# A hybrid retention and S5 step on one core: half of the input tiles transposed by DMA, and five smaller moves in the order of work

## The chip, the core and the metric

One core of one Trainium2 chip runs the whole kernel in one launch. The metric is the device time of one execution in microseconds (us), given as the median of several executions. The core has five engines, each with its own in-order queue: TensorE (PE; its weight loads are shown apart as PEld), VectorE (DVE), ScalarE (ACT), GpSimd (POOL) and SyncE (SP), which issues nearly all DMAs here. The 16 DMA engines are shared by all DMAs.

## The reference, cut to what matters

One layer of a streaming encoder. A prompt of 2048 rows and 8 x 16 sample rows, 1024 wide, give 17 tiles of 128 rows (tile 16 holds the samples).

```python
hn = rmsnorm(x, norm_g)
q, k, v, g_ret, u, g_ssm = split(hn @ w_in)            # 1024 x 3072
q, k = rotary(q), rotary(k) * 128 ** -0.5
o, ret_state = retention(q, k, v, ret_s0)              # 4 heads of 128, per-head decay
o = rmsnorm(o, ret_norm_g) * silu(g_ret)
y, ssm_state = s5(u, h0, ...)                          # 512 channels, complex diagonal state, scan
z = gelu(y)
z = z * sigmoid(z @ w_glu + b_glu)
z = z * silu(g_ssm)
out = rmsnorm(x + concat([o, z]) @ w_out, final_norm_g)
```

## The kernel before

Matrix products are made in fp16 with both operands split in a high and a low part: three matmuls (high x high, high x low, low x high) stand for one fp32 product. So each operand is first scaled, rounded to fp16 (the high part) and subtracted from its fp32 value (the low part).

**The order of the work** is written out by hand. A list `stream` holds *slots*, small packets of matmuls for TensorE, and `hook(i, f)` hangs any other work behind slot i. The loop at the end of the kernel runs through the slots, issues each and then its hooks, so a hook's number decides where its instructions stand in every engine's in-order queue. Waits between engines are put in by the framework; moving a hook changes only the order.

**The stages**, in slots:

1. Start (lines 319 to 633): loads, squares and scales of the first weights (`gu`), tiles 0 and 1 of x.
2. *u* (slots 0 to 167): `add_ug(False, gu)` computes the S5 input u, transposed, for six chunks of tiles: (0, 1), (2, 3), (4, 5), (6, 7, 8), (9 to 12), (13 to 16). Each chunk has four column blocks `cb`, each of eight slots of three matmuls over all rows of the chunk (256, 256, 256, 384, 512, 512 columns). `evac` scales a block out of PSUM into a buffer of `ubuf` (VectorE for even `cb`, ScalarE for odd) and leaves a DMA to DRAM (`ud`) that is issued some slots later; its pieces are the 4-byte columns of the chunk, 33 x 4 = 132 bytes for chunk 0, 128 for chunks 1 and 2, 192, 256 and 288 for the others.
3. Head 0 (slots 168 to 303), then the gate columns `gd` (to 495, as in stage 2, through SiLU), then heads 1 to 3 (136 slots each, to `G0` = 904). A head runs over tiles 0 to 8, 16, 9 to 15; `Step` projects a tile (eight slots of three matmuls), rotates q and k, multiplies scores with the mask into `sm` (`r2`, slot n + 17), and takes `sm` up again in `r3` (or, for the sample tile, `r3s` at n + 19 and four `state` calls from n + 20).
4. The S5 scan of 16 pairs of groups is hung between the slots from 286 on (`C1` = 304, one pair per 34 slots). It reads `ud`, keeps its tiles in the pool `s5` ("E5", "gw", "Vs", "dh" and others) and writes y to `yd`.
5. GLU (64 slots from `G0`): eight `Glu` objects, each 280 columns for all four blocks: `split` z, matmuls, `tanh` on ScalarE, `gate`.
6. Output (`Out`, lines 1423 to 1440): 17 tiles of two halves of 24 matmuls.

**The x tiles.** `Hn` loads a tile into its place in `R1a` (tiles 0 to 8) or `R1b` (9 to 16). `stat` squares it on ScalarE and takes the rsqrt on POOL; `norm` scales it in place on VectorE; each `half` transposes four 128 x 128 blocks on TensorE (L157) into PSUM, copies the high part out on ScalarE (L161) and the low part on VectorE (L162). `prep(t, i, lat)` hangs stat at slot i, norm at i + 4, the halves at i + lat and two later. Tiles 9 to 12 have their halves at slots 68 to 94, tiles 13 to 16 at 106 to 130; chunk 4 begins at slot 104, chunk 5 at 136.

**Weights.** A `Group` squares its weights (L194, L196), and `pre` (L215, VectorE), `mat` (L219, TensorE) and `fin` (VectorE) make scales of the norms; `Ws.split` makes the fp16 parts (L188, L189).

**The S5 set-up** (`s5_setup`, a generator) makes the tables of the scan: first some 200 small VectorE operations, then eight batches `b4` with matmuls into "kps" (L569) and transposes into "wps" (L584). `pump(setup)` runs one step of it; 180 calls are spread evenly over slots 20 to 290 (`SP0`), and by slot 290 it has to be done.

**Buffers.** `xp` has two tiles "x" of 128 x 1024 fp32, `ubp` four tiles "ub". In the u stage even chunks put two blocks into one "x" tile, odd chunks one block into one "ub". The gate columns and the S5 output use "ub" alone. A tile that is taken again waits for the DMA that last read it.

Of the kernel before, what the change touches and what calls it, by code (L numbers as in the profile page):

```python
# [10 lines left out]
F32 = mybir.dt.float32  # L11
# [9 lines left out]
D = 1024  # L21
NK = 8
# [40 lines left out]
def kernel(ctx: ExitStack, tc: tile.TileContext, eye, cst, rot, x_prompt, x_sample, state_ret,  # L63
# [71 lines left out]
    class Hn:  # L135
# [14 lines left out]
        def norm(self):  # L150
            V.tensor_scalar(self.x, self.x, self.s[:, 2:3], None, OP.mult)

        def half(self, q, bank="aux"):
# [473 lines left out]
    gu.square(6)  # L627
    gu.square(7, True)
    hns[1].half(0, "aux")
    gu.scale()  # L630
    hns[1].half(1, "tr")
    wu[0].split()
    wu[1].split()
# [16 lines left out]

    xh = [None]

    def ubuf(ci, cb, gate):
        if gate or ci % 2:
            return ubp.tile([128, 576], F32, tag="ub", name="ub", bufs=4)
        if cb % 2 == 0:
            xh[0] = xp.tile([128, D], F32, tag="x", name="xu", bufs=2)
        return xh[0][:, 512 * (cb % 2):512 * (cb % 2) + 512]

# [161 lines left out]
    def hook(i, f):  # L821
        hooks.setdefault(max(int(i), 0), []).append(f)
# [64 lines left out]
    for s in seq:  # L887
        n = s.at
        hook(n + 7, s.r0)
        hook(n + 15, s.r1)  # L890
        hook(n + 17, s.r2)
        if s.t < 16:
            hook(n + 23, s.r3)
            hook(n + 28, s.r4)
            hook(n + 32, s.st)
        else:
            hook(n, s.r3s_load)
            hook(n + 19, s.r3s)
            hook(n + 25, s.r3s2)
            for q in range(4):  # L900
                hook(n + 20 + 2 * q, lambda s=s, q=q: s.state(q))
            hook(n + 30, s.r4)
            hook(n + 33, s.st)
# [16 lines left out]
    hook(9, rest_smalls)  # L920
    for t, i, lat in ((4, 7, 10), (5, 12, 14), (6, 24, 22), (7, 32, 20), (8, 40, 20),
                      (9, 50, 18), (10, 58, 18), (11, 66, 18), (12, 76, 16), (13, 86, 20), (14, 96, 18), (15, 104, 18), (16, 112, 16)):
        prep(t, i, lat)
    for i in range(5):
        t, n = 4 * i, 1 if i == 4 else 4
        hook(64 + 14 * i, lambda t=t, n=n: dma(rots[:, t:t + n, :], dap(rot, t * 16384, [[128, 128], [16384, n], [1, 128]])))
# [286 lines left out]
    for i in range(1, len(groups)):  # L1213
        grp = groups[i][0]
        _, f0, l0 = groups[i - 1]
        if i == 1:
            ld, sq, sc, sp_ = 9, 46, 88, [98 + 8 * k for k in range(8)]
        else:
            ld, sq, sc, sp_ = f0 + 8, f0 + 20, f0 + 64, [f0 + 78 + 7 * k for k in range(8)]
        for k in range(8):  # L1220
            hook(ld + (4 if i == 1 else 5) * k, grp.ws[k].load)
            hook(sq + 5 * k, lambda grp=grp, k=k: grp.square(k))
            hook(sp_[k], grp.ws[k].split)
        hook(sc, grp.pre)
        hook(sc + 4, grp.mat)
        hook(sc + 6, grp.fin)
    H3 = groups[-1][1]
    pieces = [(hf, k) for k in range(NK) for hf in range(2)]
    for j, (hf, k) in enumerate(pieces):
        hook(H3 + 4 + 3 * j, wog.sq[hf][k].load)  # L1230
        hook(H3 + 14 + 3 * j, lambda hf=hf, k=k: wog.square(hf, k))
    hook(H3 + 64, wog.pre)
    hook(H3 + 68, wog.mat)
    hook(H3 + 70, wog.norms)
    for k in range(4):
        hook(H3 + 64 + 3 * k, wgl[k].load)
        hook(H3 + 76 + 3 * k, lambda k=k: gg_.square(k, k % 2))
    hook(H3 + 88, gg_.pre)
    hook(H3 + 92, gg_.mat)
# [13 lines left out]
    class Glu:  # L1253
# [3 lines left out]
        def loadg(self):  # L1257
            t = self.t
            self.g = zp.tile([128, 1120], F32, tag="i1", name="gt", bufs=3).rearrange("p (c n) -> p c n", c=4)
            dma(self.g, dap(gd, t * NCOL + 1, [[8 * NCOL, 128], [128 * 8 * NCOL, 4], [1, 280]]))  # L1260

# [23 lines left out]
        def gate(self, cb):  # L1285
            th = self.th[cb]
            z = zb[:, cb, self.t, :]
            V.scalar_tensor_tensor(th, th, 1.0, z, op0=OP.add, op1=OP.mult)  # L1288
            G.tensor_tensor(z, th, self.g[:, cb, :], OP.mult)

# [9 lines left out]
    for t in range(8):  # L1300
        if t < 6:
            hook(G0 + 8 * t + 7, glus[t + 2].split)
        hook(G0 + (1, 1, 2, 18, 25, 31, 37, 44)[t], glus[t].loadg)
    for t in range(8):
        for cb in range(4):
            n = G0 + 8 * t + 2 * cb + 1
            hook(n, lambda t=t, cb=cb: glus[t].tanh(cb))
            hook(n + (10, 9, 7, 5, 4, 3, 1, 0)[t], lambda t=t, cb=cb: glus[t].gate(cb))

    class Out:  # L1310
# [17 lines left out]
        def split(self):  # L1328
            t = self.t
            if t > 0:  # L1330
                self.split_o()
# [68 lines left out]
    for t in range(8):  # L1400
        for k in range(NK):
            def slot(t=t, k=k):
                glus[t].mmul(k)
            stream.append(slot)
    zp = None
    for i, slot in enumerate(stream):
        if i == G0:
# [3 lines left out]
        for f in hooks.pop(i, ()):  # L1411
            f()
        if 20 <= i < SP0 and (i - 20) * 180 // (SP0 - 20) != (i - 19) * 180 // (SP0 - 20):
            pump(setup)
# [6 lines left out]
    dma(fg, dap(final_g, 0, [[0, 128], [1, D]]))  # L1421

    outs[0].split()
    for t in range(17):
# [6 lines left out]
        if t == 0:  # L1431
            outs[0].part(0, 0, 512, range(4))
            outs[0].part(1, 512, 1024, range(4))
        outs[t].mmul(0, 0, 512, 0 if t else 4)
        outs[t].mmul(1, 512, 1024, 0 if t else 4)
        if t > 0:
# [34 lines left out]
```

## Time and profile before

| | |
|---|---|
| median of 3 runs | 987.54 us (986.79 to 992.88) |
| the profiled execution | 983.05 us, span of its instructions 981.3 us |
| mean granted TensorE clock | 0.982 |
| TensorE busy | 941.1 us, 96% |
| VectorE, ScalarE, GpSimd busy | 637.4, 452.2, 341.6 us |
| DMA moved | 106.17 MB |
| u stage on TensorE (first L694 to first L708) | 19.44 to 140.19 us |
| GLU on TensorE (first L1276 to first L1356) | 745.64 to 796.75 us |

Times in views are us from the start of the span. A line of the timeline reads: start, duration, engine, source line, operation, out<-in by the program's names, shape, count; in square brackets the idle time of the engine before it and who ended it. A line of groups gives busy us and mean ns after the bar, then idle time before them. A line of waits gives the sum in us, how often, and the longest. A line of stretches gives for each engine the busy us and instructions, then the granted clock (1.00 is full speed), the DMA engines' busy share (above 1 where packets queue up) and GB/s. The chain of waits is followed back from the last instruction to whatever released each one. Matmul durations are modelled and overlap; the distance of two starts is their pace.

### The profile page before, as it was taken

How to read it: one execution, taken by the hardware profiler on the slowest of the kernel's cores; microseconds unless marked ns; L12 is line 12 of the kernel's file. 1: busy time of each engine (PE TensorE's matmuls, PEld its weight loads, DVE VectorE, ACT ScalarE, POOL GpSimd, SP SyncE). 2: the span in 40 equal slices, each digit the busy share in tenths (PEclk: the TensorE clock that was granted, in tenths of full speed). 3: DMA queues.
4: the chain of work that ended last, by engine and by line, in shares of the span. 5: the costliest groups of instructions: out<-in, count | busy, mean ns of one | idle time of the engine just before them, and what ended most of it. 6: DMA issues, size and time to landing. Idle time of an engine off the chain costs nothing.

```text
span 981.3 us, 16034 instructions
## 1 busy us (share of the span) xinstructions
PE 941.1 (96%) x5414; PEld 566.8 (58%) x5414; DVE 637.4 (65%) x1544; ACT 452.2 (46%) x1150; POOL 341.6 (35%) x636
## 2 busy tenths in 40 slices
PE   5989999999989999999999999999999999999997
PEld 4865545555677555655665556565657754444444
DVE  5598654555599746775677647777465995545544
ACT  5556324333477444543545444454445754334332
POOL 1114324421354424543555434555222760000000
PEclk7989999999999999999999989999999999999999
DMA  9995354211285334211132201273264333443432
GB/s 293 231 130 93 94 117 118 76 52 50 53 161 98 98 86 112 77 56 56 37 98 73 70 26 56 86 251 123 58 192 132 103 132 108 139 130 110 153 114 86
DMA packets 145650, 106.17 MB, mean 108 GB/s; under 512 B 62192, under 2 KB 129312, under 8 KB 145056
## 3 DMA queue, kind: packets, MB, share of 16 engines
q1 hardware_dynamic: 145424, 104.88, 40.3%
q8 instruction: 43, 0.70, 0.3%
q14 instruction: 39, 0.32, 0.1%
q10 hardware_dynamic: 144, 0.26, 0.1%
HBM read 69.15 MB, written 35.96 MB: 107 GB/s over the span
## 4 chain that ended last, share of the span: by engine, by line
PE 77%; DVE 12%; ACT 3%; issue 3%; POOL 2%; DMA 2%; SPq 1%; POOLq 0%; ACTq 0%; DVEq 0%
PE pj L708 10%; PE pj L709 10%; PE pj L710 10%; PE outps L1358 6%; PE outps L1357 6%; PE outps L1356 6%; PE ups L694 5%; PE ups L696 5%; PE ups L695 5%; DVE th L1288 2%; PE yps L1068 1%; PE scps L745 1%; PE ops L769 1%; PE yps L1070 1%; PE stps L768 1%
## 5 line engine op out<-in xcount | busy, mean ns | idle before, releaser
L725 POOL TENSOR_TENSOR rot<-A,Pm 128x128 f32<-128x128 f32 x136 | 75.4, 573 | 139.7 <-DVE A L721 110.7
L708 PE MATMUL pj<-w,R1a 128*128 128x512 f16 x288 | 109.3, 380 | 0.0
L710 PE MATMUL pj<-w,R1a 128*128 128x512 f16 x288 | 109.1, 379 | 0.0
L709 PE MATMUL pj<-w,R1a 128*128 128x512 f16 x288 | 109.1, 379 | 0.0
L1358 PE MATMUL outps<-w,mh 128*128 128x512 f16 (+1 forms) x280 | 104.4, 373 | 1.6 <-DVE mh L1326 1.6
L1356 PE MATMUL outps<-w,mh 128*128 128x512 f16 (+1 forms) x280 | 104.4, 373 | 0.0
L1357 PE MATMUL outps<-w,mh 128*128 128x512 f16 (+1 forms) x280 | 104.4, 373 | 0.0
L708 PE MATMUL pj<-w,R1b 128*128 128x512 f16 x256 | 97.7, 382 | 0.0
L709 PE MATMUL pj<-w,R1b 128*128 128x512 f16 x256 | 97.3, 380 | 0.0
L710 PE MATMUL pj<-w,R1b 128*128 128x512 f16 x256 | 97.3, 380 | 0.0
L728 ACT ACTIVATE vt<-pj,hv 128x128 f32<-128x128 f32 x68 | 25.1, 370 | 133.9 <-DVE A L721 133.9
L694 PE MATMUL ups<-R1a,w 128*128 128x256 f16 (+1 forms) x256 | 75.4, 294 | 1.5 <-ACT w L188 1.3
L696 PE MATMUL ups<-R1a,w 128*128 128x256 f16 (+1 forms) x256 | 75.2, 294 | 0.2 <-DVE w L189 0.2
L695 PE MATMUL ups<-R1a,w 128*128 128x256 f16 (+1 forms) x256 | 75.3, 294 | 0.0
L1367 ACT ACTIVATE res<-xo 128x512 f32<-128x512 f32 (+1 forms) x35 | 21.7, 619 | 107.0 <-DVE xo L1366 58.2
L132 POOL TENSOR_TENSOR ss<-ss,C 128x1 f32<-128x1 f32 x68 | 15.4, 226 | 141.8 <-ACT sj L755 141.8
L758 DVE SCALAR_TENSOR_TENSOR on<-ops,ss,gg 128x128 f32<-128x128 f32 x64 | 22.4, 350 | 62.1 <-POOL ss L133 62.1
L1366 DVE SCALAR_TENSOR_TENSOR xo<-outps,ex,xo 128x512 f32<-128x512 f32 (+1 forms) x35 | 25.6, 731 | 53.6 <-PE outps L1358 53.6
L755 ACT ACTIVATE sj<-ops 128x128 bf16<-128x128 f32 x64 | 17.7, 277 | 83.8 <-PE ops L769 81.4
L132 POOL TENSOR_TENSOR fs<-fs,half__73 128x1 f32<-128x1 f32 x16 | 3.0, 189 | 151.5 <-DVE fs L1371 151.5
L189 DVE SCALAR_TENSOR_TENSOR w<-raw,gc,w 128x512 f16<-128x512 f32 x48 | 41.1, 860 | 21.7 <-ACT w L188 21.6
L696 PEld LDWEIGHTS <-w 128*128 128x128 f16 x384 | 38.2, 99 | 22.9 <-issue 0.7
(347 smaller groups left out, 2418.1 us busy)
## 6 DMA issues: line engine op xcount, KB each, us to landing
raw<-in_w_in_dram SPq DMA_DIRECT2D x48, 256.0 KB
raw<-in_w_out_dram SPq DMA_DIRECT2D x32, 256.0 KB
xo<-in_x_prompt_dram SPq DMA_DIRECT2D x16, 512.0 KB
out_dram<-res SPq DMA_DIRECT2D x16, 512.0 KB
R1a<-in_x_prompt_dram SPq DMA_DIRECT2D x9, 512.0 KB
uraw<-ud SPq DMA_DIRECT2D x32, 140.5 KB
yd<-ysb SPq DMA_DIRECT2D x32, 140.0 KB
R1a<-yd SPq DMA_DIRECT2D x4, 1120.0 KB
```

Source lines behind the costliest of these rows:

```text
L189: V.scalar_tensor_tensor(d[:, 1, :], self.raw, sc, d[:, 0, :], op0=OP.mult, op1=OP.subtract)
L694: mm(ov, w[:, 0, c], hh, start=k == 0, stop=False)
L695: mm(ov, w[:, 0, c], hl, start=False, stop=False)
L696: mm(ov, w[:, 1, c], hh, start=False, stop=k == NK - 1)
L708: mm(self.pj, hh, w[:, 0, :], start=k == 0, stop=False)
L709: mm(self.pj, hh, w[:, 1, :], start=False, stop=False)
L710: mm(self.pj, hl, w[:, 0, :], start=False, stop=k == NK - 1)
L725: G.tensor_tensor(self.rot[:, :, a, :], A[:, :, a, :], Pm[:, :, 1 - a, :], OP.add if a else OP.subtract)
L1356: mm(p, m[:, k, 0, :], w[:, 0, cw], start=k == 0, stop=False)
L1357: mm(p, m[:, k, 0, :], w[:, 1, cw], start=False, stop=False)
L1358: mm(p, m[:, k, 1, :], w[:, 0, cw], start=False, stop=k == NK - 1)
L1366: V.scalar_tensor_tensor(self.x[:, c], p, icc, self.x[:, c], op0=OP.mult, op1=OP.add)
```

## The change

1. **Tiles 9 to 16.** No norm in place and no transposes on TensorE. `halves` scales and splits the tile by rows into a tile `b` of the "x" tag (high part on ScalarE, low part on VectorE, the scale of the norm applied in both); `turn` issues one DMA on SP that transposes `b` (128 x 2048 fp16, sixteen 128 x 128 blocks) into the tile's place in `R1a` or `R1b`. Hung at stat + 4 and stat + 8; the stats are up to eight slots earlier than before.
2. **Buffers of u.** `b` takes the "x" tiles, so all u blocks go through the four "ub" tiles.
3. **Start.** `gu.scale()` stands ahead of the first transposes of tile 1, `wu[0].split()` ahead of the second ones.
4. **Set-up later.** 30 of the 180 calls between slots 20 and 104, 150 between 104 and 290.
5. **Sample step and norms.** `r3s` and the `state` calls one slot later; `pre` of the groups two to six slots earlier, apart from `mat` and `fin`.
6. **GLU and output.** The loaded gate g is multiplied by z on POOL ahead of the tanh (`zg`, two operations of 560 columns for each t), so that the gate after the tanh is one VectorE operation that writes z. g is loaded by two DMAs, for t = 0 and 1 up to 15 slots earlier into tiles of the pool `s5`. The gates are hung closer behind their tanh. Output tile 1 has its o part split and multiplied ahead, together with tile 0's, before the z parts.

```diff
+        def halves(self):
+            b = self.b = xp.tile([128, NK, 2, 128], F16, tag="x", name="xb", bufs=2)
+            xv = self.x.rearrange("p (k n) -> p k n", k=NK)
+            rs = self.s[:, 2:3]
+            act(b[:, :, 0, :], xv, AF.Copy, scale=rs)
+            V.scalar_tensor_tensor(b[:, :, 1, :], xv, rs, b[:, :, 0, :], op0=OP.mult, op1=OP.subtract)
+
+        def turn(self):
+            nc.sync.dma_start_transpose(R(self.t).rearrange("p k l n -> p (k l) n"), self.b.rearrange("p k l n -> p (k l n)"))
...
+    gu.scale()
     hns[1].half(0, "aux")
-    gu.scale()
+    wu[0].split()
     hns[1].half(1, "tr")
-    wu[0].split()
     wu[1].split()
...
     def ubuf(ci, cb, gate):
-        if gate or ci % 2:
-            return ubp.tile([128, 576], F32, tag="ub", name="ub", bufs=4)
-        if cb % 2 == 0:
-            xh[0] = xp.tile([128, D], F32, tag="x", name="xu", bufs=2)
-        return xh[0][:, 512 * (cb % 2):512 * (cb % 2) + 512]
+        return ubp.tile([128, 576], F32, tag="ub", name="ub", bufs=4)
...
-            hook(n + 19, s.r3s)
+            hook(n + 20, s.r3s)
             hook(n + 25, s.r3s2)
             for q in range(4):
-                hook(n + 20 + 2 * q, lambda s=s, q=q: s.state(q))
+                hook(n + 21 + 2 * q, lambda s=s, q=q: s.state(q))
...
-    for t, i, lat in ((4, 7, 10), (5, 12, 14), (6, 24, 22), (7, 32, 20), (8, 40, 20),
-                      (9, 50, 18), (10, 58, 18), (11, 66, 18), (12, 76, 16), (13, 86, 20), (14, 96, 18), (15, 104, 18), (16, 112, 16)):
+    for t, i, lat in ((4, 7, 10), (5, 12, 14), (6, 24, 22), (7, 32, 20), (8, 40, 20)):
         prep(t, i, lat)
+    for t, i in ((9, 50), (10, 56), (11, 62), (12, 68), (13, 80), (14, 88), (15, 96), (16, 104)):
+        hook(i, hns[t].stat)
+        hook(i + 4, hns[t].halves)
+        hook(i + 8, hns[t].turn)
...
-        hook(sc, grp.pre)
+        hook(sc - 6, grp.pre)
...
-    hook(H3 + 64, wog.pre)
+    hook(H3 + 60, wog.pre)
...
-    hook(H3 + 88, gg_.pre)
+    hook(H3 + 86, gg_.pre)
...
         def loadg(self):
             t = self.t
-            self.g = zp.tile([128, 1120], F32, tag="i1", name="gt", bufs=3).rearrange("p (c n) -> p c n", c=4)
-            dma(self.g, dap(gd, t * NCOL + 1, [[8 * NCOL, 128], [128 * 8 * NCOL, 4], [1, 280]]))
+            if t < 2:
+                self.g = [s5(tg, [128, 2, 280]) for tg in (("E5", "gw"), ("Vs", "dh"))[t]]
+            else:
+                g = zp.tile([128, 1120], F32, tag="i1", name="gt", bufs=3).rearrange("p (c n) -> p c n", c=4)
+                self.g = [g[:, 0:2, :], g[:, 2:4, :]]
+            for h, g in enumerate(self.g):
+                dma(g, dap(gd, t * NCOL + 1 + h * 256 * 8 * NCOL, [[8 * NCOL, 128], [128 * 8 * NCOL, 2], [1, 280]]))
+
+        def zg(self, h):
+            g = self.g[h]
+            G.tensor_tensor(g, g, zb[:, 2 * h:2 * h + 2, self.t, :], OP.mult)
...
         def gate(self, cb):
             th = self.th[cb]
-            z = zb[:, cb, self.t, :]
-            V.scalar_tensor_tensor(th, th, 1.0, z, op0=OP.add, op1=OP.mult)
-            G.tensor_tensor(z, th, self.g[:, cb, :], OP.mult)
+            V.scalar_tensor_tensor(zb[:, cb, self.t, :], th, 1.0, self.g[cb // 2][:, cb % 2, :], op0=OP.add, op1=OP.mult)
...
-        hook(G0 + (1, 1, 2, 18, 25, 31, 37, 44)[t], glus[t].loadg)
+        n = G0 + (-14, -12, 2, 14, 22, 30, 38, 46)[t]
+        hook(n, glus[t].loadg)
+        for h in range(2):
+            hook(n + 9 + h, lambda t=t, h=h: glus[t].zg(h))
...
-            hook(n + (10, 9, 7, 5, 4, 3, 1, 0)[t], lambda t=t, cb=cb: glus[t].gate(cb))
+            hook(n + (7, 5, 4, 3, 2, 1, 0, 0)[t], lambda t=t, cb=cb: glus[t].gate(cb))
...
+    def due(i):
+        return 30 * max(min(i, 104) - 20, 0) // 84 + 150 * max(i - 104, 0) // (SP0 - 104)
...
-        if 20 <= i < SP0 and (i - 20) * 180 // (SP0 - 20) != (i - 19) * 180 // (SP0 - 20):
+        if i < SP0 and due(i) != due(i + 1):
             pump(setup)
...
+    outs[1].split_o()
     outs[0].split()
...
         if t == 0:
-            outs[0].part(0, 0, 512, range(4))
-            outs[0].part(1, 512, 1024, range(4))
-        outs[t].mmul(0, 0, 512, 0 if t else 4)
-        outs[t].mmul(1, 512, 1024, 0 if t else 4)
+            for q in range(2):
+                outs[q].part(0, 0, 512, range(4))
+                outs[q].part(1, 512, 1024, range(4))
+        outs[t].mmul(0, 0, 512, 0 if t > 1 else 4)
+        outs[t].mmul(1, 512, 1024, 0 if t > 1 else 4)
```

More of the change, by code (lines that the diff above doesn't have):

```diff
@@ L649, in flush_store @@
             pend_store.pop(0)()
-    xh = [None]
     def ubuf(ci, cb, gate):
-        if gate or ci % 2:
-            return ubp.tile([128, 576], F32, tag="ub", name="ub", bufs=4)
-        if cb % 2 == 0:
-            xh[0] = xp.tile([128, D], F32, tag="x", name="xu", bufs=2)
-        return xh[0][:, 512 * (cb % 2):512 * (cb % 2) + 512]
+        return ubp.tile([128, 576], F32, tag="ub", name="ub", bufs=4)
     def evac(ci, cb, grp, gate, pj):
@@ L1329, in split @@
             t = self.t
-            if t > 0:
+            if t > 1:
                 self.split_o()
```

## The prediction, made before the changed kernel was timed

> **What bounds the kernel now.** I read the page, then the busy time in 5 us stretches, what TensorE waits for, and the chain of waits. The page first:
>
> ```profile
> span 981.3 us, 16034 instructions
> PE 941.1 (96%) x5414; PEld 566.8 (58%) x5414; DVE 637.4 (65%) x1544; ACT 452.2 (46%) x1150; POOL 341.6 (35%) x636
> ```
>
> TensorE is the bound nearly everywhere; 40 us of the span are idle on it. Below: busy time of PE, PEld, DVE, ACT, POOL, then granted clock, DMA share, GB/s.
>
> ```profile
> 30.00:35.00 5.00, 4.84 (x46) 4.28 (x44) 2.77 (x6) 2.59 (x5) 0.00 (x0) 1.00 0.94 335
> 35.00:40.00 5.00, 5.00 (x48) 4.41 (x46) 3.62 (x12) 3.05 (x6) 1.71 (x4) 1.00 1.02 414
> 45.00:50.00 5.00, 5.00 (x48) 4.48 (x46) 4.48 (x17) 3.08 (x6) 0.74 (x2) 1.00 1.37 51
> 60.00:65.00 5.00, 2.98 (x25) 2.51 (x26) 4.86 (x17) 2.83 (x7) 1.48 (x3) 1.00 1.04 175
> 65.70:72.50 6.80, 5.54 (x22) 3.09 (x20) 6.65 (x34) 2.06 (x5) 0.00 (x0) 0.50 1.30 80
> 80.00:85.00 5.00, 3.58 (x25) 2.32 (x24) 3.90 (x14) 2.99 (x5) 3.73 (x7) 1.00 0.40 78
> 448.00:451.40 3.40, 3.40 (x15) 3.10 (x16) 0.00 (x0) 0.78 (x3) 0.00 (x0) 0.50 0.00 0
> 574.30:581.10 6.80, 6.80 (x28) 5.57 (x27) 0.00 (x0) 1.14 (x4) 0.23 (x2) 0.50 0.00 1
> ```
>
> Three things stand there. Between 45 and 85 us VectorE is full (4.5 to 4.9 of 5) and TensorE starves. The DMA engines are full from the start to past 70 us, at first fast (414 GB/s, tiles of x), then at 51 GB/s with the short rows of the u stores. And the clock is halved for 6.8 us at 65.7, for 3.4 at 448 and for 6.8 at 574. What TensorE waits for:
>
> ```profile
> PE hnps L157 <- DVE R1a L151: 6.8, 2, 5.5
> PE nps L219 <- DVE gc L215: 5.5, 3, 2.5
> PE hnps L157 <- DVE R1a L162: 4.7, 4, 2.0
> PE ops L786 <- DVE sm L748: 3.7, 3, 1.4
> PE glps L1277 <- DVE U L1266: 1.9, 2, 1.1
> PE outps L1358 <- DVE mh L1326: 1.6, 1, 1.6
> ```
>
> So the change aims at real waits: the transposes of the x tiles behind VectorE, the norm matmuls, the sample step (L786), and the end of the GLU.
>
> **The stage of u, part by part.** It runs from 19.44 us (first L694) to 140.19.
>
> ```profile
> 19.44 0.39 PE L694 MATMUL ups<-R1a,w 128*128 128x256 f16 x1 [1.30 <-ACT w L188]
> 69.11 0.71 ACT L674 ACTIVATE xu<-ups,gc 128x256 f32<-128x256 f32 x1
> 90.37 0.57 PE kps L569 x8
> 91.53 0.22 PE wps L584 x2
> 93.91 0.44 PE hnps L157 x4
> 139.54 0.38 PE L694 MATMUL ups<-R1b,w 128*128 128x512 f16 x1
> 139.76 0.38 PE L695 MATMUL ups<-R1b,w 128*128 128x512 f16 x1
> 140.19 0.38 PE L708 MATMUL pj<-w,R1a 128*128 128x512 f16 x1
> ```
>
> *Removed:* tiles 9 to 16 need no TensorE transposes: 8 tiles x 2 halves x 0.44 us = 7.0 us. *VectorE and ScalarE per tile:*
>
> ```profile
> L151 DVE TENSOR_SCALAR R1b<-R1b,xs 128x1024 f32<-128x1024 f32 x8 | 5.9, 742 | 0.0
> L162 DVE TENSOR_TENSOR R1b<-hnps,R1b 128x512 f16<-128x512 f32 x16 | 10.9, 684 | 4.8 <-ACT R1b L161 4.8
> L161 ACT ACTIVATE R1b<-hnps 128x512 f16<-128x512 f32 x16 | 9.6, 597 | 23.1 <-PE hnps L157 23.1
> L147 ACT ACTIVATE Sst<-R1b 128x1024 bf16<-128x1024 f32 x8 | 8.4, 1052 | 0.0
> L1266 DVE SCALAR_TENSOR_TENSOR U<-R1a,ex,U 128x1120 f16<-128x1120 f32 x8 | 12.1, 1508 | 0.5 <-ACT U L1265 0.4
> ```
>
> Out go 0.742 + 2 x 0.684 = 2.11 us of VectorE, in comes one split of 1024 (L1266's 1120 in 1.51, so about 1.38): 0.7 us a tile less, 6 us in all. ScalarE gives 1.19 and takes about 1.05. By itself that is worth nothing except where VectorE is full, and there the set-up helps more: 30 calls of it run by slot 104 where 84 x 180/270 = 56 did.
>
> *Check of the working on before:* from the end of chunk 2 (69.11 + 0.71 = 69.8) to 140.2 are 70.4 us. A 512-column matmul takes 0.216 (139.54 to 139.76), so chunk 3 needs 4 x 24 x 0.162 = 15.6 and chunks 4 and 5 need 8 x 24 x 0.216 = 41.5: 57.1. Fourteen half-tiles of transposes (6.2), four set-up batches of 0.57 + 2 x 0.22 = 1.0 (4.0), the 1.4 us wait in 80 to 85 and half of the 2.7 us left at half clock (1.35) make 70.1. It closes, so I use the same sum for after: 57.1 + three batches (3.0) + 0.6 = 60.7 us.
>
> *Where chunk 2 ends after.* Here the change adds a wait. Before, the u stores of even chunks lay in the x buffers and those of odd ones in four "ub" tiles, so a buffer came round after eight stores; now after four, since x is needed for the split tiles.
>
> ```profile
> 29.27 3.42 SPq L141 DMA_DIRECT2D R1b<-in_x_prompt_dram  x7
> 35.67 10.71 SPq L686 DMA_DIRECT2D ud<-xu  x4
> 37.93 0.67 DVE L676 TENSOR_SCALAR ub<-ups,gc 128x256 f32<-128x256 f32 x1
> 61.59 0.67 SPq L686 DMA_DIRECT2D ud<-ub  x1
> R1b<-in_x_prompt_dram SPq DMA_DIRECT2D x7, 512.0 KB
> ud<-xu SPq DMA_DIRECT2D x4, 132.0 KB
> 285.66 4.97 DMA gd<-ub
> ```
>
> Eight tiles of x (4.2 MB, 0.5 MB more behind them) issued from 29.3 take until about 42 at 335 to 414 GB/s. Then chunk 0's four stores, 0.53 MB at 51 GB/s, land one per 2.6 us: 44.6, 47, 50, 52. Chunk 1's first evacuation, at 37.93 before, must wait for 44.6; VectorE stands behind it, and TensorE, with two banks, stops from about 38.5 to 45. That this happens with four buffers shows in the gate's columns, where the chain holds 4.97 us of "gd<-ub". The store pipe is full either way, so its times stay: chunk 1's last store, issued at 61.6, lands at about 65, and chunk 2 ends at 66 instead of 69.8. Then 66 + 60.7 = 126.7, 13.5 us before 140.2. I give 2 back for the transposing DMAs standing between the stores on SP's queue: **-11.5**. Bounds: -3 (if every buffer waits that much longer) to -15.
>
> The earlier scale lets w's first split start before the second half of tile 1, about 1.8 us sooner. I count **0**: the buffer wait at 44.6 swallows it (bounds -2.5 and 0).
>
> The Trainium skill, "TensorE: Matmul & The Clock Gate", Part 1, says that the clock falls to half after an idle window of about 3.4 us. Here it fell at 448 after a wait of only 1.4 us (L786), so the trace is stricter; by either, the stop at 38.5 to 45 brings half clock, which the bound of the store pipe hides.
>
> *Transposing DMAs.* No row shows one. Each moves 512 KB: 1.3 us at 414 GB/s, 10.3 us at 51 GB/s. Its pieces are short rows, nearest to the mix of 128- and 512-byte rows at 175 GB/s: 3.0 us; I take **4**. The first is issued at about 61, the fourth must be there when chunk 4 begins, at about 82, the eighth at about 103: at 4 us each they are there at 77 and 93, hidden. SP stands while it waits for the split; behind it are u stores and tables of positions, due later. ScalarE's split of a tile waits for the transpose two before (two x buffers); that is in the 2 us.
>
> For these DMAs the Trainium skill has two answers: "Advanced Engine Details and Errata", X-Bar Transpose, has them as fast as plain ones, which would leave my sum; "VectorE: DVE Perf Modes", The three transpose paths, has 1309 ns for 128x128, and sixteen blocks one after another would be an estimated 21 us a tile and some 110 us lost. No run here shows which.
>
> **Later parts.** *Set-up moved back:* (98 - 81)/13 = 1.3 batches go from u into head 0, where TensorE is full: **+1.0** (0 to 2). *Sample step one slot later:* three waits of 1.0 to 1.4 us shrink by a slot of three matmuls, 0.65 us each: **-2.0** (0 to -3.7). If the halved stretches at 448 and 574 go too, that is half of 3.4 + 6.8 = -5.1; the wait of 1.0 us below halved nothing, so a wait of 0.7 may not either; which way is open, so I take half, **-2.6** (0 to -5.1).
>
> ```profile
> 218.13 0.49 PE L786 MATMUL ops<-sm,vt 128*128 128x128 f32 x2 [1.03 <-DVE sm L748]
> ```
>
> *pre earlier:* the 1.4 us wait at 83 to 85 is in the u sum; the 2.5 us one at 289 lies behind the store wait at 285.66, so **0** (0 to -2.5).
>
> *GLU and output.* POOL's product moves ahead of the tanh, two wide ones a tile for four:
>
> ```profile
> L1289 POOL TENSOR_TENSOR R1a<-th,gt 128x280 f32<-128x280 f32 x32 | 34.6, 1101 | 11.3 <-DVE th L1288 11.3
> L1288 DVE SCALAR_TENSOR_TENSOR th<-th,R1a 128x280 f32<-128x280 f32 x32 | 23.7, 785 | 0.0
> 746.15 0.89 POOL L132 TENSOR_TENSOR ss<-ss,C 128x1 f32<-128x1 f32 x1 [4.11 <-ACT sj L755]
> ```
>
> VectorE's 32 gates stay, POOL's last products no longer trail them, and the 1.9 and 1.6 us waits should lose about 2.5. Output row 1's half ahead gives TensorE 24 more matmuls of cover. Against it: four of the new products (4 x 2 x 0.92 to 1.1, some 8 us) stand on POOL from five slots before the GLU, and the rsqrt at 746.15 queues behind them; its transposition four slots later waits about 1.5 us. **-1.0** (+3 to -4). Two loads of g for one on SP cost nothing: SP waits there.
>
> **The sum.** -11.5 + 1.0 - 2.0 - 2.6 - 1.0 = -16.1. The profiled execution took 983.05 us (span 981.3), so 967; it lay 4.5 under the median of the three runs (987.54), so **971.5** as such a median.
>
> **Rivals.** *Store pipe wins.* The transposes and the four buffers delay each chunk; u gains 3 instead of 11.5, 980. For it: DMA share above 1 from 35 to 72 us. Against: 0.40 at 80 to 85. *Slower: turning at the rate of short rows.* At 10 us each the fourth is there at 101 (due 82) and the eighth at 141 (due 122 by then), so TensorE stops 19 us twice, u ends at 165 instead of 140, and the whole takes 987.5 + 25 - 4.6 = 1008. It decides from about 8 us a tile, where 61 + 8 x 8 + 21 = 146 eats the other terms. For it: 51 GB/s is what 132-byte rows get; against: 175 with 512-byte ones. (The block-by-block figure of the Trainium skill belongs here.) *Better:* u -15, both halved stretches gone (-5.1), sample -2, GLU -3.5, +1: 963.
>
> **How the numbers follow.** Forecast 0.52, better 0.16, store pipe 0.19, slow turning 0.13. 1% (10 us) is about what a measurement of this kernel can tell from no change. Faster by more: 0.68; within: 0.19; slower: 0.13. The range leaves out a little below "better" and most of slow turning: 957 to 994. The likeliest case alone: 965 to 977.
>
> **What would show it.** u's last matmul before head 0 at about 127; a stop of TensorE at 38 to 45 ended by a "ud<-ub" landing; no stop at chunk 4's start; waits of L786 under 0.8 us; "outps <- mh" gone. Wrong if the first matmuls of chunk 4 or 5 wait on R1b's DMA, or if no store wait shows at 38 (then u ends earlier still).

## The result and the profile after

The changed kernel takes 976.3 us (median of four, 972.64 to 978.0) against 987.16 for the kernel before (986.67 to 992.88): ratio 0.9872 with an interval of 0.9826 to 0.9918. Measured a second time beside other runs of the kernel before, it gave 978.09 against 990.07, 0.9865 (0.9821 to 0.991). It is faster by 1.3%, inside the range and the forecast's own 965 to 977, but most of the gain did not come from where the largest term put it.

The top of the page after:

```profile
span 970.9 us, 15913 instructions
PE 927.3 (96%) x5350; PEld 556.1 (57%) x5350; DVE 631.3 (65%) x1528; ACT 448.1 (46%) x1142; POOL 337.4 (35%) x620
```

TensorE is busy for 14 us less (941.1 to 927.3) and the span is 10.4 us shorter: the share stays 96%. So what it no longer does is paid for, in part, by new idle time. To place it I cut both profiled executions at the first matmul of each stage (columns in us; the fourth to the ninth are lengths):

| kernel | u begins | head 0 begins | head 0 | gate | head 1 | head 2 | head 3 | GLU | output to end | span |
|---|---|---|---|---|---|---|---|---|---|---|
| before | 19.4 | 140.2 | 117.9 | 109.1 | 124.6 | 128.9 | 125.0 | 51.1 | 184.5 | 981.3 |
| after | 16.9 | 136.6 | 119.5 | 109.3 | 121.6 | 124.2 | 126.0 | 51.0 | 182.7 | 970.9 |

Head 0 begins 3.6 us earlier, heads 1 and 2 together are 7.7 shorter, the output 1.8; head 0 and head 3 give back 1.6 and 1.0. Each row is one execution, and the stage of u varies between executions: head 0 begins at 143.3 us in b_step below, whose u is that of the kernel before, and at 138.0 and 140.2 in after_again and a_noglu, whose u is that of the changed kernel. A difference of 2 to 3 us in u therefore says little by itself.

What TensorE waits for, after:

```profile
PE ups L698 <- DVE ub L680: 12.3, 3, 10.9
PE nps L229 <- DVE gc L225: 5.6, 1, 5.6
PE ups L698 <- DVE zf L417: 3.3, 1, 3.3
PE glps L1292 <- ACT gg L738: 2.7, 1, 2.7
PE ops L773 <- DVE sm L752: 1.9, 1, 1.9
PE hnps L167 <- DVE R1a L151: 1.2, 1, 1.2
```

The three waits of the sample step, the waits on transposed x tiles but one of 1.2 us, and "outps <- mh" are gone. ("ops L773" is another step at the end of head 3, taken up below.) New at the top is a wait on a "ub" evacuation: three times, 10.9 us at the longest. The stretches around it (PE, PEld, DVE, ACT, POOL busy, granted clock, DMA share, GB/s):

```profile
35.00:40.00 5.00, 3.63 (x34) 3.19 (x32) 0.23 (x1) 1.19 (x2) 0.83 (x2) 1.00 1.03 414
40.00:45.00 5.00, 0.00 (x0) 0.00 (x0) 0.00 (x0) 0.00 (x0) 0.00 (x0) 0.72 1.09 259
45.00:50.00 5.00, 0.47 (x3) 0.33 (x3) 1.17 (x3) 0.00 (x0) 0.00 (x0) 0.50 1.50 53
50.00:55.00 5.00, 5.00 (x36) 4.08 (x35) 2.33 (x6) 3.12 (x6) 0.74 (x2) 0.75 1.16 131
70.00:75.00 5.00, 1.70 (x16) 1.24 (x15) 4.38 (x16) 4.07 (x8) 0.74 (x2) 1.00 1.08 195
```

From 40 to 45 us no engine does anything, while the DMA engines are full. TensorE stops from 38.6 to 49.5, and then works half clocked (0.75 over 50 to 55; the records show half clock from 42.2, 3.6 us into the stop, for 10.2 us). That agrees with the Trainium skill, "TensorE: Matmul & The Clock Gate", Part 1, whose idle window of about 3.4 us is well exceeded here. The chain of waits, VectorE's timeline and SP's timeline name the reason:

```profile
36.80 14.99 DMA ud<-ub
```

```profile
48.83 0.65 DVE L680 TENSOR_SCALAR ub<-ups,gc 128x256 f32<-128x256 f32 x1 [13.60 <-DMA ud<-ub]
```

```profile
35.51 10.24 SPq L690 DMA_DIRECT2D ud<-ub  x4
45.80 4.03 SPq L193 DMA_DIRECT2D raw<-in_w_in_dram  x2
```

Chunk 1's first evacuation waits 13.60 us for the store of chunk 0 that holds its buffer, and all VectorE work stands behind it. The wait is the one that was forecast. It is longer: the buffer is free at 48.8 us, not at 44.6. Behind the four stores SP, itself held for 10.24 us (10.71 in the kernel before), brings the next weights late too.

The second stop, 3.3 us up to 74.8 ("zf L417" in the waits above), has another reason. The first matmul of chunk 3 waits for VectorE to empty its PSUM bank:

```profile
70.45 1.28 DVE L158 SCALAR_TENSOR_TENSOR xb<-R1b,xs,xb 128x1024 f16<-128x1024 f32 x1 [0.35 <-ACT xb L157]
71.66 1.01 DVE L429 TENSOR_SCALAR zf<-zf 128x16 f32<-128x16 f32 x6
73.50 0.68 DVE L172 TENSOR_TENSOR R1a<-hnps,R1a 128x512 f16<-128x512 f32 x1
74.10 0.65 DVE L680 TENSOR_SCALAR ub<-ups,gc 128x256 f32<-128x256 f32 x1
```

That evacuation (L680) waits for no store: it stands in VectorE's queue behind a split, set-up operations and a low part.

The transposing DMAs and the splits, in the views of their line and of tile R1b (shortest, median and longest in ns; then first and last start, us):

```profile
L161 SPq DMA_TRANSPOSE R1b<-xb x8: 1727/2225/3456, 68.1 to 100.7; - x8
```

```profile
L157 ACT ACTIVATE xb<-R1b,xs x8: 1133/1148/1151, 65.6 to 95.6; 128x1024 f16<-128x1024 f32 x8
L158 DVE SCALAR_TENSOR_TENSOR xb<-R1b,xs,xb x8: 1275/1279/1285, 66.8 to 99.4; 128x1024 f16<-128x1024 f32 x8
```

The splits cost 1.15 and 1.28 us (estimates 1.05 and 1.38); a transpose holds SP for 1.7 to 3.5 us. No wait of TensorE for a DMA into R1b shows; ScalarE's splits wait for one 0.41 us here, and more in some of the runs below.

### The profile page after: what moved, and what is told of

It reads as the page before. It is cut to its first block, busy times and chain, and to the rows that moved or that the text cites. A ratio compares the mean times of both kernels' runs of the same rounds, so it can differ in the third digit from the quotient of the medians.

```text
span 970.9 us, 15913 instructions
## 1 busy us (share of the span) xinstructions
PE 927.3 (96%) x5350; PEld 556.1 (57%) x5350; DVE 631.3 (65%) x1528; ACT 448.1 (46%) x1142; POOL 337.4 (35%) x620
## 4 chain that ended last, share of the span: by engine, by line
PE 79%; DVE 8%; DMA 4%; POOL 3%; ACT 3%; issue 2%; SPq 1%; POOLq 0%; ACTq 0%; DVEq 0%
PE pj L712 11%; PE pj L714 11%; PE pj L713 11%; PE outps L1375 6%; PE outps L1374 6%; PE outps L1373 6%; PE ups L698 4%; PE ups L700 4%; PE ups L699 4%; PE scps L749 2%; DMA ud<-ub 2%; PE glps L1292 1%; PE glps L1293 1%; PE glps L1294 1%; PE ops L773 1%
## 5 line engine op out<-in xcount | busy, mean ns | idle before, releaser
L729 POOL TENSOR_TENSOR rot<-A,Pm 128x128 f32<-128x128 f32 x136 | 75.3, 573 | 123.4 <-DVE A L725 102.3
L712 PE MATMUL pj<-w,R1a 128*128 128x512 f16 x288 | 109.3, 380 | 0.0
L714 PE MATMUL pj<-w,R1a 128*128 128x512 f16 x288 | 109.1, 379 | 0.0
L713 PE MATMUL pj<-w,R1a 128*128 128x512 f16 x288 | 109.1, 379 | 0.0
L698 PE MATMUL ups<-R1a,w 128*128 128x256 f16 (+1 forms) x256 | 74.8, 292 | 15.9 <-DVE ub L680 10.9
L1384 ACT ACTIVATE res<-xo 128x512 f32<-128x512 f32 (+1 forms) x35 | 21.6, 617 | 104.4 <-DVE xo L1383 58.2
L132 POOL TENSOR_TENSOR ss<-ss,C 128x1 f32<-128x1 f32 x68 | 16.1, 236 | 137.8 <-ACT sj L759 137.8
L762 DVE SCALAR_TENSOR_TENSOR on<-ops,ss,gg 128x128 f32<-128x128 f32 x64 | 22.4, 350 | 61.8 <-POOL ss L133 61.8
L132 POOL TENSOR_TENSOR fs<-fs,half__73 128x1 f32<-128x1 f32 x16 | 3.0, 189 | 157.7 <-DVE fs L1388 157.7
```

The lines of the kernel that those rows point to most:

```text
L698: mm(ov, w[:, 0, c], hh, start=k == 0, stop=False)
L712: mm(self.pj, hh, w[:, 0, :], start=k == 0, stop=False)
L713: mm(self.pj, hh, w[:, 1, :], start=False, stop=False)
L714: mm(self.pj, hl, w[:, 0, :], start=False, stop=k == NK - 1)
L729: G.tensor_tensor(self.rot[:, :, a, :], A[:, :, a, :], Pm[:, :, 1 - a, :], OP.add if a else OP.subtract)
```

## The experiments

Theory: the gain lies in the sample step and the halved clock; the transposing DMAs are cheap; the four store buffers stop TensorE in chunk 1 and cost what the transposes save. Rivals: the gain is the transposes'; the stop is covered by the store pipe (the queue of u's stores in the DMA engines) anyway, so buffers do not matter; or VectorE's backlog sets u's end. (The expectations call it the "lag theory" that the wait for a buffer delays all that follows.)

**b_four**: the kernel before with four store buffers, nothing else.

```
 def ubuf(ci, cb, gate):
-    if gate or ci % 2:
-        return ubp.tile([128, 576], F32, tag="ub", name="ub", bufs=4)
-    if cb % 2 == 0:
-        xh[0] = xp.tile([128, D], F32, tag="x", name="xu", bufs=2)
-    return xh[0][:, 512 * (cb % 2):512 * (cb % 2) + 512]
+    return ubp.tile([128, 576], F32, tag="ub", name="ub", bufs=4)
```

> The kernel before with one edit: all u blocks go through the four ub tiles, as after. Lag theory (the wait for a buffer four stores back costs the u stage about what the DMA transposes win): TensorE stops some 11 us at about 38 us behind VectorE's evacuation, ended by a landing of ud<-ub, the clock is halved once, chunk 3 starts at 74 us or later instead of 68.9, and the time is 5 to 9 us over before. Rival (the stop of after comes from the transposing DMAs on SP's queue): no stop over 3 us near 38, and a time within 2 us of before.

Measured: 1005.94 against 993.32, 1.0111 (1.0043 to 1.018). Head 0 begins at 154.2 instead of 140.2.

```profile
PE ups L688 <- DVE ub L670: 10.1, 1, 10.1
```

The buffers make the stop by themselves, and it is not covered: what the store pipe held in the kernel before ran beside TensorE's work, what it holds here does not.

**b_step**: the kernel before with only the sample step moved.

```
-            hook(n + 19, s.r3s)
+            hook(n + 20, s.r3s)
...
-                hook(n + 20 + 2 * q, lambda s=s, q=q: s.state(q))
+                hook(n + 21 + 2 * q, lambda s=s, q=q: s.state(q))
```

> The kernel before with one edit: r3s and the state calls of the sample tile one slot later. Clock theory: the waits of L786 on sm fall from 3.7 us to under 2 in sum and the halved clock after them in heads 1 and 2 goes too, so heads 1 and 2 take 121 to 125 us each instead of 124.6 and 128.9, and the time is 4 to 7 us below before. Rival: only the waits shrink, the clock is still halved there; 1 to 2 us.

Measured: 980.86 against 993.32, 0.9881 (0.9834 to 0.9929): some 12 us for one slot, more than the 4 to 7 expected. The whole change has 0.9872, so this one move is worth as much as all six parts together, within their intervals. The same two stretches, first of the kernel before, then of this one:

```profile
440.00:460.00 20.00, 18.61 (x94) 11.38 (x92) 9.80 (x27) 8.68 (x24) 6.50 (x12) 0.91 0.10 28
560.00:580.00 20.00, 18.61 (x99) 13.27 (x98) 11.30 (x28) 8.76 (x26) 7.85 (x17) 0.86 0.07 21
```

```profile
440.00:460.00 20.00, 19.97 (x114) 12.42 (x113) 12.89 (x32) 10.14 (x30) 8.24 (x18) 1.00 0.15 42
560.00:580.00 20.00, 19.98 (x120) 12.94 (x118) 15.09 (x36) 11.60 (x33) 9.12 (x18) 1.00 0.21 60
```

TensorE's idle 1.39 us is gone from each, and the clock is whole: 114 matmuls where 94 went. In every kernel here with the shift head 1 takes 121.5 or 121.6 us and head 2 124.2 to 124.3. The mean clock of the runs measured together here has a median of 0.979 for the kernel before (0.974 to 0.984) and of 0.987 for this one (0.985 to 0.988); 0.8% of 981 us is some 8 us, so by this estimate more than half of the 12 is clock. Head 0 is less clear: without the shift the traces of the kernel before, b_four and b_turn have 10.2, 20.5 and 17.1 us of half clock in heads 0 to 2; of the eleven traces with it nine have none, but after_again has 3.4 us at 221.4 and a_pe_zx 6.8 at 215.2, both in head 0 and with no wait of TensorE over 0.71 us there.

**a_pe**: the changed kernel with tiles 9 to 16 transposed on TensorE and the x tiles as store buffers again, as before; all other parts stay.

```
 def ubuf(ci, cb, gate):
-    return ubp.tile([128, 576], F32, tag="ub", name="ub", bufs=4)
+    if gate or ci % 2:
+        return ubp.tile([128, 576], F32, tag="ub", name="ub", bufs=4)
...
+                      (9, 50, 18), (10, 58, 18), (11, 66, 18), (12, 76, 16), (13, 86, 20), (14, 96, 18), (15, 104, 18), (16, 112, 16)):
...
-    for t, i in ((9, 50), (10, 56), (11, 62), (12, 68), (13, 80), (14, 88), (15, 96), (16, 104)):
-        hook(i, hns[t].stat)
-        hook(i + 4, hns[t].halves)
-        hook(i + 8, hns[t].turn)
```

> The changed kernel with tiles 9 to 16 transposed on TensorE as before and the buffers of u as before; start, set-up, sample step, pre, GLU and output as after. Lag theory: no stop near 38; TensorE does 7 us more of transposes, VectorE 6 us more; head 0 starts at 130 to 135 us (136.6 after), the time is 0 to 6 us below after. Rival (the transposing DMAs carry the gain): the waits of hnps on VectorE come back, head 0 starts at 139 or later, the time is 3 us or more over after.

Measured: 973.65 against 993.32, 0.9808 (0.976 to 0.9855), the lowest ratio of the four kernels measured together. Its interval overlaps those of the changed kernel (0.9872 and 0.9865), so by itself it leaves open whether the transposes cost or win. Its u takes 117.6 us where the changed kernel's takes 119.7 (121.0 in after_again, and 123.4 in a_noglu, whose u is the same).

**b_turn**: the other side, the kernel before with the transposing DMAs and the four buffers alone (`halves`, `turn`, their hooks, and `ubuf` as in b_four).

> The kernel before with parts 1 and 2 of the change alone: tiles 9 to 16 split in rows and turned by DMAs, all u blocks in four ub tiles. Theory now (the buffers cost more than the transposes win): the 10 us stop near 40 us and the wait on sm of the sample step both stand; head 0 starts at 142 to 150 us, between the 140 of before and the 154 of the kernel with four buffers alone, and the time is 0 to 8 us over before. Rival (the transposes do carry part of the gain): 3 us or more under before.

Measured: 996.93 against 990.07, 1.0051 (1.0025 to 1.0077): slower. Head 0 begins at 148.7 us, and the waits of the sample step stand (3.7 us), as expected.

```profile
PE ups L698 <- DVE ub L680: 11.7, 1, 11.7
PE ups L698 <- ACT ub L678: 7.4, 1, 7.4
```

The first stop is the one on a store: VectorE's evacuation waits 14.37 us for "ud<-ub". The second, up to 83.0, is not: there the evacuation on ScalarE starts without a wait for a store, behind a split that waited 2.40 us for POOL's rsqrt. So the part that gives the change its name loses about 5 us by the ratio (2.5 to 7.6). Against b_four the DMAs themselves win some 0.6%, but the two intervals overlap.

**a_mixed**: the changed kernel with chunk 0 in the two x tiles and all others in "ub", so that chunk 1 finds free buffers.

```
-    return ubp.tile([128, 576], F32, tag="ub", name="ub", bufs=4)
+    if gate or ci:
+        return ubp.tile([128, 576], F32, tag="ub", name="ub", bufs=4)
+    if cb % 2 == 0:
+        xh[0] = xp.tile([128, D], F32, tag="x", name="xu", bufs=2)
+    return xh[0][:, 512 * (cb % 2):512 * (cb % 2) + 512]
```

> The changed kernel with one edit: chunk 0's four u blocks lie in the two x tiles as before the change, all others in the four ub tiles (the x tiles are free again when the first split tile needs one). Lag theory: the 11 us stop at 38 us goes, chunk 2 starts at about 48 instead of 58, chunk 3 at about 68 instead of 75, and the time falls 5 to 9 us below after, to about 969. Rival (the store pipe sets the pace whatever the buffers): the stop only moves to chunk 2, chunk 3 starts at 72 to 75 and the time stays within 2 us of after.

Measured: 977.87 against 993.32, 0.9857 (0.98 to 0.9913), no measurable difference from the changed kernel. Chunk 2 begins at 45.4 us instead of 58.2, but chunk 3 at 72.1 instead of 74.8. The long waits and VectorE's timeline:

```profile
PE hnps L167 <- DVE R1a L172: 8.6, 1, 8.6
```

```profile
59.01 0.65 DVE L686 TENSOR_SCALAR ub<-ups,gc 128x256 f32<-128x256 f32 x1 [9.39 <-DMA ud<-ub]
```

The stop only moved, as the rival had it: the first buffer that comes round again, now in chunk 2, waits 9.39 us, and 12.8 us won at chunk 2's start are 2.7 at chunk 3's. That the store pipe itself sets chunk 3's start is not shown. Here too the last wait before it ends with an evacuation (71.43 us) that waits for no store and stands behind a split and the set-up in VectorE's queue. Against a_pe, measured beside it and without transposing DMAs, a_mixed is slower: a_pe's slowest run (975.04) lies under its fastest (975.93).

**a_latex**: the changed kernel, with the x tiles 13 to 16 loaded later, so that chunk 0's stores meet less traffic.

```
-    for t in range(9, 17):
+    for t in range(9, 13):
         hns[t].load()
+    for t in range(13, 17):
+        hook(22 + 4 * (t - 13), hns[t].load)
```

> The changed kernel with one edit: tiles 13 to 16 of x are loaded behind chunk 0's stores (slots 22 to 34) and not ahead of them, 2 MB less in their way. If the x tiles ahead of them make chunk 0's stores late, the stop near 38 shrinks from 10.9 us to 4 to 7 and chunk 2 starts 4 to 6 us sooner (58.2 after), the time falls by 2 to 5 us if the pipe does not take it back in chunk 2. Rival (the slow 132-byte rows alone make them late): the stop stays at 9 us or more and the time within 1 us.

Measured: 980.21 against 990.07, 0.9876 (0.9833 to 0.992), beside 978.09 of the changed kernel, measured with it.

```profile
PE ups L698 <- DVE ub L680: 8.6, 4, 5.6
PE ups L698 <- DVE zf L417: 5.0, 1, 5.0
```

```profile
69.08 8.01 DMA R1b<-xb
```

The longest stop falls from 11.5 in the run of the changed kernel beside it to 5.6, so the x tiles are part of what makes the stores late. The difference comes back as smaller stops: chunk 2 begins at 53.9 instead of 58.8, chunk 3 at 72.3 instead of 75.4, chunk 4 at 95.2 instead of 92.9. One cause is in the chain of waits: the first transposing DMA, which now meets the later x tiles, lands only after 8.01 us, and ScalarE waits 7.45 us for it before its next split.

**a_latew** and **a_lateb_w**: the changed kernel with head 0's weights loaded later; the second of them also with chunks 0 and 2 in the x tiles and the transposes later.

```
-            ld, sq, sc, sp_ = 9, 46, 88, [98 + 8 * k for k in range(8)]
+            ld, sq, sc, sp_ = 40, 66, 108, [116 + 7 * k for k in range(8)]
```

```
-    return ubp.tile([128, 576], F32, tag="ub", name="ub", bufs=4)
+    if gate or ci not in (0, 2):
+        return ubp.tile([128, 576], F32, tag="ub", name="ub", bufs=4)
...
-    for t, i in ((9, 50), (10, 56), (11, 62), (12, 68), (13, 80), (14, 88), (15, 96), (16, 104)):
+    for t, i in ((9, 70), (10, 75), (11, 80), (12, 85), (13, 96), (14, 102), (15, 108), (16, 114)):
```

> The changed kernel with one edit: head 0's weights are loaded, squared, scaled and split later (loads at slots 40 to 68 instead of 9 to 37), so that 2 MB in 512-byte pieces no longer stand between the u stores of chunks 0 and 1 on the DMA queue. Store-pipe theory (the landing of u's stores sets the pace of chunks 1 and 2, the buffers only pass it on): the 11 us stop near 38 shrinks by under 2 us, since the tiles of x stand ahead of chunk 0's stores and not the weights, but chunk 3 starts 2 to 5 us sooner after the stop than the 16.6 us of after (58.2 to 74.8), 2 to 5 us off the time. Rival (VectorE, or the splits of tiles 9 to 12, sets the pace after the stop): chunk 2 still takes 16 us or more, time within 1.5 us of after.

> The changed kernel with head 0's weights later, chunks 0 and 2 of u in the x tiles again, and the splits and transposing DMAs of tiles 9 to 16 moved to slots 74 to 122, when those tiles are free. Store-pipe theory: no stop over 3 us at 38 to 60, and TensorE is rid of 7 us of transposes; head 0 starts at 122 to 128 us (136.6 after), the time is 6 to 12 us below after, 964 to 970. Rival (the transposing DMAs come too late or too slowly): TensorE waits at the start of chunk 4 on a DMA into R1b, head 0 starts at 134 or later.

Measured against 994.58: 983.46, 0.9906 (0.9875 to 0.9937), and 985.94, 0.9943 (0.991 to 0.9975). Both ratios lie above the changed kernel's 0.9872 and 0.9865, and a_lateb_w's interval only touches theirs; a_noglu, measured with them and like the changed kernel up to the GLU, has 977.93. Both expectations failed. In a_latew the stop near 38 stays (10.9 us) and chunk 2 still takes 16.5 us, which was the sign of the rival; but chunk 4 begins at 99.9 us instead of 91.5, and the chain of waits shows why:

```profile
69.98 12.53 DMA R1b<-xb x2
83.11 8.44 DMA R1b<-xb
```

The weights now load at the time of the transposes, which then take some 6 to 8 us; ScalarE's splits wait 3.57, 2.98 and 5.63 us for them, and the evacuations stand behind. In a_lateb_w chunk 3 does begin at 60.7 us, 14 earlier than in the changed kernel, but chunk 4 at 100.2, 8.7 later, and head 0 at 146.5, where 122 to 128 was expected:

```profile
PE ups L704 <- DVE ub L686: 5.1, 1, 5.1
PE ups L704 <- ACT ub L684: 5.0, 1, 5.0
PE ups L704 <- ACT xu L684: 4.4, 1, 4.4
```

```profile
34.84 17.00 DMA ud<-xu
76.39 7.55 DMA ud<-xu
86.54 4.36 DMA R1b<-xb
```

Three stops of 4.4 to 5.1 us at evacuations take the place of one of 10.9. Ahead of the evacuations ScalarE stands 8.73 us for a late weight, then 6.21 and 4.93 us for stores that still hold the x tiles in which the splits are made. The last row is also the shortest transpose, from issue to landing, in any chain here: 4.36 us, where the estimate was 4. The longest is the 8.44 above.

**a_pe_even**: a_pe with the set-up spread as before the change.

```
-        return 30 * max(min(i, 104) - 20, 0) // 84 + 150 * max(i - 104, 0) // (SP0 - 104)
+        return 180 * max(i - 20, 0) // (SP0 - 20)
```

> The kernel with transposes and u buffers as before and the rest of the change, with one more edit: the set-up spread evenly over slots 20 to 290 again. If the later set-up is what freed VectorE, the waits of hnps on VectorE come back, the u stage takes 121 to 125 us instead of 117.6 and head 0 about 1.5 us less than 119.5; the time rises by 2 to 5 us. If not, u stays within 1.5 us and the time too.

Measured: 978.48 against 994.58, 0.9859 (0.9798 to 0.992). In the profiles u is 8.1 us longer than in a_pe (125.7 and 117.6) and head 0 2.6 shorter (116.9 and 119.5): moving the set-up out of u is worth some 5 us net, by the profiles and by the two ratios (0.9808 and 0.9859), though the two were not measured together and their intervals overlap. Where the 8.1 lie:

```profile
PE hnps L167 <- DVE R1a L172: 7.6, 5, 2.9
```

In a_pe the same wait comes to 4.5 us in two pieces, so 3.1 of the 8.1 are there: VectorE has more of the set-up in front of the low parts (L172). The clock, halved for 13.7 us in this u and for 3.4 in a_pe's, has its share in the rest.

**a_noglu**: the changed kernel with the gate product behind the tanh, and its loads and hooks, as before.

```
-            V.scalar_tensor_tensor(zb[:, cb, self.t, :], th, 1.0, self.g[cb // 2][:, cb % 2, :], op0=OP.add, op1=OP.mult)
+            z = zb[:, cb, self.t, :]
+            V.scalar_tensor_tensor(th, th, 1.0, z, op0=OP.add, op1=OP.mult)
+            G.tensor_tensor(z, th, self.g[:, cb, :], OP.mult)
...
```

> The changed kernel with the GLU part undone (g loaded whole, product with g on POOL after the gate, old hooks); the early o part of output tile 1 stays. Theory: POOL's early products delay the rsqrt and rotation of head 3's last steps, so without them head 3 takes about 125.0 instead of 126.0 us, the wait of 2.7 us at the start of the GLU goes, the wait of 1 to 2 us on the output's split stays hidden by the early part; GLU within 1 us of 51.0: total 0 to 2 us less than after. Rival: the product ahead pays, and the time is 2 us or more over after.

Measured: 977.93 against 994.58, 0.9859 (0.9785 to 0.9933): no difference in the median. But the stages part: head 3 takes 124.6 us (126.0 in the changed kernel), the output 184.5 (182.7).

```profile
PE glps L1284 <- DVE U L1273: 1.9, 2, 1.1
```

The waits of 1.9 and 2.7 us around the end of head 3 are gone and the two short ones of the kernel before are back in the GLU; the output's wait, expected to stay hidden, is back too (below). What the product gains in the output it loses on POOL.

**after_again**, the changed kernel once more, and **a_pe_zx**: a_pe with the loads of a_latex and the products of tiles 0 and 1 later on POOL.

```
-            hook(n + 9 + h, lambda t=t, h=h: glus[t].zg(h))
+            hook(n + (16, 18, 9, 9, 9, 9, 9, 9)[t] + h, lambda t=t, h=h: glus[t].zg(h))
```

> The changed kernel itself once more, beside the others on one chip: a ratio to before of 0.984 to 0.990; a pair of 121.6 and 124.2 us for heads 1 and 2.

> A version meant to beat both kernels: transposes and u buffers as before the change, the rest of the change, tiles 13 to 16 of x loaded behind chunk 0's stores, and POOL's first two products z times g some 7 and 9 slots later, behind head 3's last rsqrt and rotation. Theory: u takes 112 to 117 us (117.6 without the later loads), head 3 about 124.6 to 125 instead of 126, the output 182.7 as after; 967 to 972 on a chip where before takes 990, 0.976 to 0.981 of it. Rival (u's length is set elsewhere, and the products then come too late for the gate): within 1 us of the kernel without these two edits, 0.981.

Measured: 978.09 (977.46 to 981.22) and 966.31 (963.52 to 969.41) against 990.07: 0.9865 (0.9821 to 0.991) and 0.9731 (0.9678 to 0.9784). The second beats both kernels, by 11.8 us the changed one beside it, without any transposing DMA. Its longest waits:

```profile
PE nps L229 <- DVE gc L225: 5.2, 1, 5.2
PE hnps L167 <- DVE R1b L172: 2.8, 3, 1.6
PE ups L704 <- ACT ub L682: 2.2, 2, 1.5
PE wps L594 <- ACT zf L584: 1.4, 2, 0.7
```

```profile
40.00:45.00 5.00, 5.00 (x48) 4.39 (x47) 4.49 (x15) 2.63 (x6) 1.28 (x3) 1.00 1.72 40
45.00:50.00 5.00, 5.00 (x49) 4.57 (x47) 2.61 (x8) 3.86 (x8) 0.74 (x2) 1.00 1.29 85
```

Where the changed kernel stands still TensorE is full, though the DMA engines still work at 40 GB/s: with eight blocks of buffers and the later loads the store pipe is nearly hidden (the longest wait for an evacuation is 1.5 us). u takes 115.1 us, head 3 124.7, the GLU 49.8, the output 182.7. Its two edits on top of a_pe were not run apart.

## Why the prediction was right, and where it was not

**The step that failed is u, -11.5.** Measured in the profiles, head 0 begins 3.6 us earlier (start and u together). The cause was named, a buffer freed by chunk 0's store, and the end of u after chunk 2 was sized well: from chunk 3's first matmul at 74.8 to 136.6 are 61.8 us, where 60.7 and 2 were forecast. What was wrong is "chunk 2 ends at 66". It assumed that chunk 0's stores free their buffers in turn, as their bytes fit at 51 GB/s behind x (44.6, 47, 50, 52). The bytes did fit: by the trace's packet records the stores' packets ran from 42.8 to 53.0 us. But three quarters of them were done at 47.4 and no buffer was free before 48.8; the second came at 51.9. (Chunk 1's other two evacuations, at 55.9 and 58.5, waited for no store.) So the first buffer came 4.2 us later than forecast, half clock over the first 2.9 us of work after the stop cost some 1.5, and VectorE's queue stopped TensorE for 3.3 at 71.5: about the 8.8 us by which chunk 3 came late. I had the sentence "the store pipe is full either way, so its times stay" as the reason why the stop costs nothing: b_four shows it false, since the same pipe with eight buffers lets TensorE work on. For u the size of the rival "store pipe wins" (-3) was right, though its reason, that every chunk is delayed by stores, holds for the first stop alone; for the whole its 980 was not right. One row was also read too widely: VectorE is at 3.90 of 5 in 80 to 85 us, not at 4.5 to 4.9 up to 85.

**The sample step and the clock were sized too low.** Forecast -4.6, measured -7.7 in the two heads of the profiles, and some 12 us in the median of b_step. The waits did not shrink by 0.65 us but went, and the halved clock with them, which I had counted by half: two waits of 1.35 and half of the 10.2 us at half clock are 7.8. The profile of the kernel before, at 983.05 us, was quicker than every timed run of it, with a clock of 0.982 where 0.979 was the median beside b_step. So its rows showed less half clock than a usual execution has, and the median gains more than they could say.

**The rest.** Set-up: +1.6 in head 0 against +1.0, but u gains more from it than I counted (a_pe_even: net some 5 us). In the forecast that gain was part of the one term for u, as one batch less and a freer VectorE, and it went down with the term. Start: u begins 2.5 us earlier (1.8 estimated) and is swallowed by the stop, as forecast. GLU and output: 360.6 us in head 3, GLU and output before, 359.7 after: -0.9 against -1.0, by the two halves foreseen. POOL's timeline of the changed kernel shows the price:

```profile
733.37 1.82 POOL L1276 TENSOR_TENSOR gw<-gw,R1a 128x560 f32<-128x560 f32 x1
735.15 2.45 POOL L1276 TENSOR_TENSOR Vs<-Vs,R1a 128x560 f32<-128x560 f32 x1
737.56 1.82 POOL L1276 TENSOR_TENSOR dh<-dh,R1a 128x560 f32<-128x560 f32 x1
739.34 1.27 POOL L132 TENSOR_TENSOR ss<-ss,C 128x1 f32<-128x1 f32 x1
```

The rsqrt (L132) starts as the last product ends, and where the products stand elsewhere (a_noglu, a_pe_zx) the waits of 1.9 and 2.7 us (L773, L1292) are gone or down to 0.7. The 1.8 us won in the output comes with the product ahead of the tanh, since in a_noglu the wait is back although the early half of output tile 1 stays:

```profile
PE outps L1365 <- DVE mh L1333: 1.6, 1, 1.6
```

**The sum.** Profiles: -3.6 + 1.6 + 0.2 (gate) - 7.7 - 0.9 = -10.4; forecast -16.1. Two errors of opposite sign, 7.9 too much for u and 3.1 too little for the heads, leave most of the difference. That the total came so near was in part luck.

**The transposing DMA** was sized at the lower end of what came: 4 us against 4.36 to 8.44. The Trainium skill, "VectorE: DVE Perf Modes", The three transpose paths, gives 1309 ns for 128x128; taken sixteen times it would be 21 us a tile, and even the 8.44 us of a_latew refute that sum: the blocks do not add up. "Advanced Engine Details and Errata", X-Bar Transpose, is nearer, and for the changed kernel the rival "slow turning" is out: no matmul of chunk 4 or 5 waited on R1b's DMA. Where other loads fell into the same time (a_latex, a_latew) the transposes did reach the 8 us from which it was to decide, and they held TensorE by way of ScalarE's splits.

## What to carry to other kernels

Before a buffer is given to something new, work out when it comes back round: a full transfer queue that nobody waits for is free, and the same queue with half the buffers stops every engine. A wait of one microsecond on a clocked engine can cost several by the clock, so a move of one slot may be worth more than a transfer of work to another unit. And size a change against the usual execution: a profile that happens to be a quick one hides clock losses.

## What the runs showed of the hardware

The clock fell to half after waits of 1.4 us in heads 1 and 2 of the kernel before, and moving one instruction group by a slot kept it whole there (20 us stretches at 0.91 and 0.86, then at 1.00). A wait of that length is not needed, though: in head 0 of after_again and a_pe_zx the clock fell with no wait over 0.71 us. Four stores issued one behind the other did not free their buffers in turn: with three quarters of their packets done at 47.4 us the first buffer came at 48.8 and the second at 51.9, where bytes over rate gave 44.6 and 47. One DMA issue on SP took 2.6 us (10.24 for four) where the queues were full. A transposing DMA of 512 KB took 4.36 us, and 8.44 beside loads of weights. Not settled: why a kernel's clock is halved in one execution and not in another at the same place, and whether the transposes pay with eight store buffers besides the x tiles, which was not tried (a_lateb_w shares the x tiles and lost).
